# A hybrid decoder layer on one core: plain blocks by thirds of the tokens, and four PSUM banks for small results

## The chip, the cores and the metric

The kernel runs on one core of a Trainium2 chip. A core has five engines that run side by side: TensorE (PE in the profile; its weight loads are listed apart as PEld), VectorE (DVE), ScalarE (ACT), GpSimd (POOL) and SyncE (SP), which here only issues transfers. Matmul results go to PSUM, which has eight banks of 512 fp32 values for each of 128 partitions; DVE or ACT read them from there into SBUF. The metric is the device time of one execution in microseconds, as the median of repeated runs. Before the change it is 2419.35 us (three runs, 2418.73 to 2423.1).

## The reference

One layer of a decoder for 1024 prompt tokens and 8 sample tokens, 1032 columns in all, with a model width of 1024. Three mixers read one normalized input through one combined projection; their gated sum is merged, and a SwiGLU block follows.

```
sc_b, sc_c, sc_x, z, xbc, dt_raw, q, gates = jnp.split(xn @ w_in, splits, axis=-1)
...
y_a = (sc_b * conv_u) @ w_sc_out
...
y_ssd, ssm_new = ssd_fn(xs, dt, a, bm, cm, ssm_s0)
...
y_b = group_rmsnorm(y_ssd, ssm_norm_w, SSM_GROUPS) @ w_ssm_out
qh = q.reshape(bsz, seq, ATTN_HEADS, ATTN_HEAD_DIM)
scores = jnp.einsum('blhd,bmhd->bhlm', qh, mem_k).astype(jnp.float32) * (ATTN_HEAD_DIM ** -0.5)
probs = jax.nn.softmax(scores, axis=-1).astype(mem_v.dtype)
y_c = jnp.einsum('bhlm,bmhd->blhd', probs, mem_v).reshape(bsz, seq, ATTN_DIM) @ w_attn_o
g_a, g_b, g_c = jnp.split(jax.nn.sigmoid(gates), N_BRANCHES, axis=-1)
merged = g_a * y_a + g_b * y_b + g_c * y_c
return merged @ w_merge_o, (sc_new, ssm_conv_new, ssm_new)
```

`ssd_fn` is a chunked scan over eight chunks of 128 tokens for the prompt and one recurrent step for the sample. The memory attention has 4 heads of width 256 over 256 memory tokens.

## The kernel before

**Blocks.** A block is one group of 128 output features for all 1032 columns, over eight groups of 128 inputs. Operands are split into a high part in the fast format fp32r and the rest (`hi`, `lo`), so a block takes three products for each of the eight inputs: hi x hi, hi x lo, lo x hi. Most large products use a Strassen scheme on halves of the tokens. The *plain* blocks use `gemm` (L199): for each input k and each of the three products, three matmuls go to three PSUM banks, with 260, 512 and 260 columns (`thirds`, L80). One block is thus 72 matmuls into one tile of three banks. The tile comes from `mm_ps` (L63), a pool of two such tiles: six banks. When all inputs are through, one instruction reads all 1032 columns.

**Small results.** The other two banks belong to the pool `psm`, from which `sm_ps` (L66) hands out one bank at a time in turn. All small matmuls and transposes of the scan, of the attention and of the norms use it.

**The stage around the change.** After the projections (span position 979 us) come 40 plain blocks in this order: eight for q (`q_step`, L868; weights named wq0 to wq7), eight each for the outputs 0, 1 and 2 (`out_part`, L1501; wo00 to wo07, wo10 to wo17, wo20 to wo27: w_sc_out and the two halves of w_ssm_out), and eight for w_attn_o (loop from L1854; wo30 to wo37). The scan of four groups runs beside q and the first outputs, the attention and the state outputs beside the rest. They are cut into pieces that stand in a queue, and `tick` (L183) inside `gemm` takes the next piece at marks spread over the eight inputs. So PE gets small work between the matmuls of a block.

In the scan, a piece of `first` (L1046) fills the tiles bp and xp, `second` (L1072) po and py, `third` (L1099) pss. (The blocks of the outputs are also called po in the profile, at L218.) In the attention, `kv_keys` fills pskT, `a_scores` psa, `a_probs` psp, `a_out` psv, `s_out` pso, and `conv_state` pcs. All of them are tiles of `sm_ps`.

**What reads a block.** For q, ACT scales the result into an SBUF tile (L872). For output 0, DVE multiplies it by a gate (L1517); for output 1, ACT copies it (L1521) and issues its store; for output 2, DVE adds what output 1 left (L1524) and multiplies by the gate (L1525). For w_attn_o, DVE multiplies by the gate (L1872) and adds to `merged` (L1873).

**Seams.** Outputs 0, 1, 2 and w_attn_o read different inputs. In the last block before each such change a callback, `between` (L1494), loads the next inputs and splits them (L177 on ACT, L178 on DVE; tiles b00h, b00l to b07h, b07l) as the old ones come free; `out_in` (L1480) does the rest in front of the first block. The tiles are shared with the inputs in use and with those of the scan: twelve for the high parts and twelve for the low ones.

**What sets the order.** Within each engine instructions run in one fixed order. It is laid out when the program is built: a scheduler takes, of those instructions that it estimates to be ready, the first in program order, and it hands out the tiles of a pool as they come free in its estimate. On the chip, an engine waits at an instruction whose input or tile is not ready, and all that follows on that engine waits with it.

**After the blocks.** The merge products begin (loop L1967, matmuls at L1949). For the pair m = 0 the tiles pa and pb are three-bank tiles of `mm_ps` and pc is made of two small banks (`pieces`, L1939, against `whole`, L1935); `onto` (L1954) adds a product to x2, with one DVE instruction for `whole` and two for `pieces`.

Of the kernel before, what the change touches and what calls it, by code (L numbers as in the profile page):

```python
# [9 lines left out]
F32 = mybir.dt.float32  # L10
# [7 lines left out]
P = 128  # L18
# [25 lines left out]
def tile_kernel(ctx: ExitStack, tc, a, o):  # L44
# [18 lines left out]
    def mm_ps(name):  # L63
        return pmm[0].tile([P, NCH, 512], F32, tag="mm", name=name)

    def sm_ps(name):  # L66
        return psm.tile([P, 512], F32, tag="sm", name=name)

    def dram(name, shape):
        return dp.tile(shape, F32, tag=name, name=name)  # L70
# [6 lines left out]
    def flat(ps):  # L77
        return ps.rearrange("p n c -> p (n c)")[:, 252 : 252 + TT]
# [120 lines left out]
    def gemm(w, acts, name, width=P, off=0):  # L199

        hi, lo = w
        ps = mm_ps(name)
        nk = len(acts)
        n = int(pace[0] + pace[1])
        pace[1] += pace[0] - n
        marks = [nk * i // n for i in range(n)]
        between = seam.pop() if seam else None
        for k, (ah, al) in enumerate(acts):
            if between is not None:
                between(k)  # L210
            if k == 1 and owed:
                owed.pop()()
            for _ in range(marks.count(k)):
                tick()
            ks = slice(k * width + off, k * width + off + P)
            for i, (wt, x) in enumerate(((hi, ah), (hi, al), (lo, ah))):
                for po, xc in thirds(ps, x):
                    PE.matmul(po, wt[:, ks], xc, start=(k == 0 and i == 0), stop=(k == nk - 1 and i == 2))  # L218
        return ps

    def wblock(w, col):
        return w[:, col : col + P].rearrange("(k p) c -> p k c", p=P)
# [585 lines left out]
    def proj(col, name):  # L808
        return gemm(weights(wblock(w_in, col), "w" + name), xn, "ps_" + name)
# [57 lines left out]

    def q_step(i):  # L868
        def s():
            ps = proj(C_Q + i * P, f"q{i}")  # L870
            t = ev_tile(f"q{i}")
            S.activation(t[:, :TT], flat(ps), AF.Copy, scale=QS)  # L872
            G.tensor_copy(qs[:, i, :], t[:, T:TT])
            S.dma_start(q_d[i], t[:, :TT])

        return [Step(wblock(w_in, C_Q + i * P), f"wq{i}", s)]
# [581 lines left out]
    st_stack.close()  # L1458
    pa_stack.close()
    ch_stack.close()  # L1460
    pmm[0] = mm_stack.enter_context(tc.tile_pool(name="pmm1", bufs=2, space=PSUM))

# [38 lines left out]
    def out_part(i, m, w, src, nxt):  # L1501


        nm = f"{i}{m}"
        if m == 0:
            out_in(src)
        if i != 1:
            gt = ev_tile(f"gt{nm}")
            SY.dma_start(gt[:, :TT], gt_d[(0, 8, 8)[i] + m])
        if i == 2:  # L1510
            t = ev_tile(f"yr{nm}")
            SY.dma_start(t[:, :TT], yr_d[m])
        if m == KD - 1:
            out_ahead(nxt)
        ps = gemm(weights(wblock(w, m * P), f"wo{nm}"), acts, f"po{nm}")
        if i == 0:
            V.tensor_mul(gt[:, :TT], flat(ps), gt[:, :TT])  # L1517
            owed.append(lambda: SY.dma_start(mg_d[m], gt[:, :TT]))
        elif i == 1:
            t = ev_tile(f"yr{nm}")  # L1520
            S.copy(t[:, :TT], flat(ps))  # L1521
            S.dma_start(yr_d[m], t[:, :TT])
        else:
            V.tensor_tensor(t[:, :TT], flat(ps), t[:, :TT], op=ALU.add)  # L1524
# [313 lines left out]
    def form_t2(kt):  # L1838
        t1, b12, b21, b22 = quarters(kt)
        V.tensor_sub(t1, t1, b22)  # L1840
        mform("nT2", kt, t1)
# [9 lines left out]
        mform("T4", kt, t2)  # L1851

    wm = [wblock(a["w_merge_o"][0], m * P) for m in range(KD)]
    for m in range(KD):  # L1854
# [17 lines left out]
        V.tensor_mul(gt[:, :TT], flat(ps), gt[:, :TT])  # L1872
        V.tensor_add(merged[m], merged[m], gt[:, :TT])  # L1873
        if m < 4:
            form_t1(m)
# [90 lines left out]
    S.activation(ln1, ones[:, 0:1], AF.Ln)  # L1966
    for m in (0, 2):  # L1967
        nm = f"wm{m}"
        raw1, raw2, sa, wA, wS = begun if m == 0 else st_begin(wm[m], wm[m + 1], nm, ev_sums)
# [456 lines left out]
```

## Time and profile before

| What | Value |
|---|---|
| Median of three runs | 2419.35 us (2418.73 to 2423.1) |
| The profiled execution | 2420.07 us |
| Its span, first to last instruction | 2418.3 us |
| Mean granted clock of PE | 0.998 |
| Scan beside plain blocks | 979 to about 1335 us |
| Attention beside plain blocks | about 1335 to 1560 us |
| Rest of w_attn_o alone | to 1643 us |

A row of the waits names an engine, what it was about to run, what it waited for, and then the total in us, the number of times and the longest wait. A row of the chain of waits is a start, a length and the work that set the end at that time. A row of a tile lists an engine's instruction on that tile with its count, its shortest, median and longest duration in ns, and the starts of the first and the last. A row of the timeline is a start, a duration, an instruction, and in brackets the idle time before it with what ended it. In names, buffer numbers are left out, and the part behind the arrow is what is read.

### The profile page before, as it was taken

The page shows a single profiled execution, that of the slowest core. Times are in us where ns is not written, and L with a number is a line of the kernel's source. Part 1 is how long each engine was busy: PE and PEld are TensorE (multiplying, and loading weights), DVE is VectorE, ACT ScalarE, POOL GpSimd, SP SyncE. Part 2 cuts the span into 40 slices and gives each one's busy share as a digit, 9 for nine tenths or more (in the row PEclk, how much of TensorE's full clock was granted, in tenths as well). Part 3 has the DMA queues.
Part 4 walks back from the last instruction along what each step waited for, and adds up shares of the span by engine and source line. Part 5 has one row for each costly group of instructions (what it writes and reads, how often), then busy time and mean ns, then how long its engine had stood idle before and what let it go on. Part 6 is the DMA issues. An engine that isn't in the chain of part 4 may idle for free.

```text
span 2418.3 us, 45032 instructions
## 1 busy us (share of the span) xinstructions
PE 2386.4 (99%) x18620; PEld 2268.5 (94%) x18620; DVE 1644.9 (68%) x2666; ACT 1098.9 (45%) x1762; POOL 106.0 (4%) x163
## 2 busy tenths in 40 slices
PE   8999999999999999999999999999999999999998
PEld 6999999999999999888888887899999999999998
DVE  6744677777777676568688773469687655567965
ACT  6633555455453543656555542214553333343423
POOL 0000000000000000212112000000000000000000
PEclk9999999999999999999999999999999999999999
DMA  6444423444354345768886796764345333355622
GB/s 210 132 154 161 136 83 115 141 141 132 108 160 118 106 132 171 231 214 271 261 283 216 255 338 222 269 231 145 117 160 174 98 102 105 93 179 154 194 90 78
DMA packets 348244, 403.74 MB, mean 167 GB/s; under 512 B 16014, under 2 KB 269054, under 8 KB 348031
## 3 DMA queue, kind: packets, MB, share of 16 engines
q1 hardware_dynamic: 324902, 337.60, 45.0%
q10 hardware_dynamic: 23137, 63.26, 6.9%
q8 instruction: 146, 2.39, 0.4%
q14 instruction: 59, 0.48, 0.1%
HBM read 284.65 MB, written 116.38 MB: 166 GB/s over the span
## 4 chain that ended last, share of the span: by engine, by line
PE 91%; DVE 3%; DMA 3%; ACT 1%; issue 1%; SPq 0%; DVEq 0%; ACTq 0%
PE po L218 12%; PE ps_q L218 3%; PE pd L2237 1%; PE pss L1103 1%; PE py L1090 1%; PE ps_z L218 1%; DMA in<-yb_d 1%; PE po L1082 1%; PE G16m L269 1%; PE d00m L269 1%; PE Z2m L269 1%; PE Z14m L269 1%; PE G22m L269 1%; PE X18m L269 1%; PE Z8m L269 1%; PE Z10m L269 1%
## 5 line engine op out<-in xcount | busy, mean ns | idle before, releaser
L1034 ACT ACTIVATE r<-r,acum 128x128 f32<-128x128 f32 x256 | 79.3, 391 | 3.3 <-DMA r<-ac_d 2.4
L823 DVE SCALAR_TENSOR_TENSOR ax<-u,prm,ax 128x1024 f32<-128x1024 f32 x44 | 56.3, 1280 | 0.0
L975 ACT ACTIVATE st<-st,es 128x128 f32<-128x128 f32 x128 | 41.4, 392 | 21.1 <-DMA st<-in_state_ssm_dram 16.6
L1067 POOL TENSOR_TENSOR xdd<-xdt,decst 128x512 f32<-128x512 f32 x32 | 34.4, 1074 | 284.1 <-DVE xdt L1063 278.3
L1061 DVE TENSOR_TENSOR r<-r,cbm 128x1024 f32<-128x1024 f32 x32 | 39.1, 1223 | 4.3 <-ACT r L1036 2.4
L1086 DVE TENSOR_TENSOR y<-po,ea 128x512 f32<-128x512 f32 x28 | 19.3, 690 | 31.6 <-PE po L1082 31.6
L977 DVE SCALAR_TENSOR_TENSOR st<-sr,dts,st 128x128 f32<-128x128 f32 x128 | 40.4, 347 | 0.4
L1524 DVE TENSOR_TENSOR yr<-po,yr 128x1032 f32<-128x1032 f32 x8 | 9.9, 1232 | 40.6 <-PE po L218 40.6
L1103 PE MATMUL pss<-xdd,bT 128*128 128x512 f32 x64 | 34.4, 619 | 2.3 <-ACT bT L1060 1.8
L981 DVE SCALAR_TENSOR_TENSOR sr<-st,sr 128x128 f32<-128x128 f32 x128 | 35.4, 286 | 1.1
L1090 PE MATMUL py<-r,xdt 128*64 128x128 f32 x512 | 35.0, 279 | 0.0
L1036 ACT ACTIVATE r<-r 128x1024 f32<-128x1024 f32 x32 | 33.8, 1057 | 0.7
L1116 POOL TENSOR_TENSOR s<-s,cdec 128x512 f32<-128x512 f32 x28 | 33.2, 1186 | 0.6 <-DVE s L1109 0.4
L1090 PEld LDWEIGHTS py<-r,xdt 128*64 128x64 f32 x512 | 27.3, 136 | 4.4 <-issue 1.0
L1082 PE MATMUL po<-bc,s 128*128 128x128 f32 x224 | 29.6, 275 | 0.0
L1082 PEld LDWEIGHTS po<-bc,s 128*128 128x128 f32 x224 | 28.0, 191 | 1.0
L1639 ACT ACTIVATE pr<-psa,mx 128x256 f32<-128x256 f32 x32 | 14.9, 471 | 30.4 <-DVE mx L1637 30.4
L826 DVE SCALAR_TENSOR_TENSOR ax<-u,prm,ax 128x1032 f32<-128x1032 f32 x22 | 28.3, 1287 | 0.0
L820 ACT ACTIVATE ax<-u,prm 128x1024 f32<-128x1024 f32 x22 | 27.4, 1246 | 1.2 <-ACT u L902 0.4
L1063 DVE TENSOR_TENSOR xdt<-xp,dtT 128x512 f32<-128x512 f32 x32 | 21.9, 684 | 8.8 <-PE xp L1056 8.8
L1627 DVE SCALAR_TENSOR_TENSOR kc<-kc,qb 128x256 f32<-128x256 f32 x64 | 23.7, 418 | 4.7 <-DMA qb<-qs_d 4.7
L1060 ACT COPY bT<-bp 128x128 f32<-128x128 f32 x32 | 8.4, 261 | 38.8 <-DVE cbm L1058 38.7
(8855 smaller groups left out, 8937.9 us busy)
## 6 DMA issues: line engine op xcount, KB each, us to landing
r<-ac_d SPq DMA_DIRECT2D x32, 512.0 KB
gt_d<-G ACTq DMA_DIRECT2D x24, 516.0 KB
gt<-gt_d SPq DMA_DIRECT2D x24, 516.0 KB
xs_d<-ax ACTq DMA_DIRECT2D x22, 516.0 KB
zs<-zs_d SPq DMA_DIRECT2D x16, 516.0 KB
yb_d<-x SPq DMA_DIRECT2D x16, 516.0 KB
in<-yb_d SPq DMA_DIRECT2D x16, 516.0 KB
st<-in_state_ssm_dram SPq DMA_DIRECT2D x32, 256.0 KB
```

The source lines that it names most:

```text
L218: PE.matmul(po, wt[:, ks], xc, start=(k == 0 and i == 0), stop=(k == nk - 1 and i == 2))
L269: last_mm[0] = PE.matmul(po, wt[:, ks], xc, start=(start and kt == 0 and i == 0), stop=(kt == 3 and i == 2), skip_group_check=True,).ins
L823: V.scalar_tensor_tensor(acc[:, :T], u[:, j : j + T], w[j], acc[:, :T], op0=ALU.mult, op1=ALU.add)
L975: S.activation(st[:, i], st[:, i], AF.Copy, scale=es[:, g * 4 + i, b : b + 1])
L977: V.scalar_tensor_tensor(st[:, i], rb, dts[:, g * 4 + i, b : b + 1], st[:, i], op0=ALU.mult, op1=ALU.add)
L981: V.scalar_tensor_tensor(rb, st[:, i], 1.0, rc, op0=ALU.mult, op1=ALU.mult, accum_out=ys[:, g * 4 + i, b : b + 1],)
L1034: S.activation(r[:, j, :], r[:, j, :], AF.Relu, scale=-1.0, bias=acum[:, c, h : h + 1])
L1061: V.tensor_tensor(r, r, bc(cbm.unsqueeze(1), [P, HPG, P]), op=ALU.mult)
L1067: G.tensor_tensor(b3(xdd, HPG), b3(xdt, HPG), bc(decst[:, c, hs].unsqueeze(2), [P, HPG, 64]), op=ALU.mult)
L1082: PE.matmul(po[:, t * P : (t + 1) * P], state["s"][:, t * P : (t + 1) * P], bcg[1][:, cs], start=True, stop=True,)
L1090: PE.matmul(py[hp : hp + 64, (h // 2) * P : (h // 2 + 1) * P], xdt[:, h * 64 : (h + 1) * 64], r[:, (h % 2) * 4 + h // 2, :], start=True, s ...
L1103: PE.matmul(pss, bT, xdd, start=True, stop=True)
```

## The change

The plain blocks of q, of the three outputs and of w_attn_o go through a new function, `gemm3`. It takes one tile of one bank for each third of 344 columns, from a pool of four banks, and calls `out` for a third as soon as all its inputs are through. With `lag` at its default of 8 the thirds run one after the other; with a lag of 1 they run side by side, each one input behind the one before. The lag is 1 in the first and last block of each output and in the first of w_attn_o. Ticks are spread over 24 steps in place of eight, and `between` is called in front of the steps of the last third. The two banks that are left go to a second small pool, and `sm_ps` alternates between both.

What reads a block now does so by thirds. In the last block of w_attn_o, the addition of yg, the first weights of the merge and six of its forms are issued from the callback of the first third. For the pair m = 0 of the merge, pa is made of the two old small banks; then the plain pools are closed, and a pool of two three-bank tiles gives pc and pb. For m = 2, pa is a three-bank tile and pc is made of small banks, as before, with pc now taken together with pa.

```diff
+    ring = {"main": None, "small": None, "n": 0}
+
     def sm_ps(name):
-        return psm.tile([P, 512], F32, tag="sm", name=name)
+        ring["n"] += 1
+        pool_ = ring["small"] if ring["small"] is not None and ring["n"] % 2 else psm
+        return pool_.tile([P, 512], F32, tag="sm", name=name)
+
+    def plain_pools(n):
+        for key, bufs in (("main", 4), ("small", 2)):
+            ring[key] = mm_stack.enter_context(tc.tile_pool(name=f"p{key}{n}", bufs=bufs, space=PSUM))
...
+    def gemm3(w, acts, name, out, lag=KD):
+
+        hi, lo = w
+        nk = len(acts)
+        pss = [ring["main"].tile([P, 512], F32, tag="mm", name=f"{name}_{t}")[:, :CW] for t in range(NCH)]
+        n = int(pace[0] + pace[1])
+        pace[1] += pace[0] - n
+        marks = [NCH * nk * i // n for i in range(n)]
+        between = seam.pop() if seam else None
+        order = [(t, m - t * lag) for m in range(nk + (NCH - 1) * lag) for t in range(NCH) if 0 <= m - t * lag < nk]
+        for step, (t, k) in enumerate(order):
+            if between is not None and t == NCH - 1:
+                between(k)
+            if step == 3 and owed:
+                owed.pop()()
+            for _ in range(marks.count(step)):
+                tick()
+            ks = slice(k * P, (k + 1) * P)
+            c = slice(t * CW, (t + 1) * CW)
+            ah, al = acts[k]
+            for i, (wt, x) in enumerate(((hi, ah), (hi, al), (lo, ah))):
+                PE.matmul(pss[t], wt[:, ks], x[:, c], start=(k == 0 and i == 0), stop=(k == nk - 1 and i == 2))
+            if k == nk - 1:
+                out(t, c, pss[t])
...
-            ps = proj(C_Q + i * P, f"q{i}")
             t = ev_tile(f"q{i}")
-            S.activation(t[:, :TT], flat(ps), AF.Copy, scale=QS)
+            gemm3(
+                weights(wblock(w_in, C_Q + i * P), f"wq{i}"), xn, f"ps_q{i}",
+                lambda n, c, ps: S.activation(t[:, c], ps, AF.Copy, scale=QS),
+            )
...
-    pmm[0] = mm_stack.enter_context(tc.tile_pool(name="pmm1", bufs=2, space=PSUM))
+    plain_pools(1)
...
-        ps = gemm(weights(wblock(w, m * P), f"wo{nm}"), acts, f"po{nm}")
+        if i == 1:
+            t = ev_tile(f"yr{nm}")
+
+        def part(n, c, ps):
+            if i == 0:
+                V.tensor_mul(gt[:, c], ps, gt[:, c])
+            elif i == 1:
+                S.copy(t[:, c], ps)
+            else:
+                V.tensor_tensor(t[:, c], ps, t[:, c], op=ALU.add)
+
+        gemm3(weights(wblock(w, m * P), f"wo{nm}"), acts, f"po{nm}", part, 1 if m in (0, KD - 1) else KD)
...
-        ps = gemm(w, acts, f"po3{m}")
-        V.tensor_add(merged[m], merged[m], yg[:, :TT])
-        if m == KD - 1:
-            begun = st_begin(wm[0], wm[1], "wm0", ev_sums)
-            for kt in range(3):
-                form_t2(kt)
-            for kt in range(3):
-                mform("B21", kt, merged[kt + 4][:, HS[0]])
-        V.tensor_mul(gt[:, :TT], flat(ps), gt[:, :TT])
+
+        def part(n, c, ps):
+            if n == 0:
+                V.tensor_add(merged[m], merged[m], yg[:, :TT])
+                if m == KD - 1:
+                    begun.append(st_begin(wm[0], wm[1], "wm0", ev_sums))
+                    for kt in range(3):
+                        form_t2(kt)
+                    for kt in range(3):
+                        mform("B21", kt, merged[kt + 4][:, HS[0]])
+            V.tensor_mul(gt[:, c], ps, gt[:, c])
+
+        gemm3(w, acts, f"po3{m}", part, KD if m else 1)
...
-        pa, pb = (whole(mm_ps(nm + n)) for n in "ab")
-        pc = pieces(nm + "c")
+        if m == 0:
+            ring["small"] = None
+            pa = pieces(nm + "a")
+        else:
+            pa, pc = whole(mm_ps(nm + "a")), pieces(nm + "c")
         m_prod(pa, wA, 0, "B11", True)
         onto(m, 0, pa)
+        if m == 0:
+            mm_stack.close()
+            pmm[0] = mm_stack.enter_context(tc.tile_pool(name="pmm2", bufs=2, space=PSUM))
+            pc = whole(mm_ps(nm + "c"))
+        pb = whole(mm_ps(nm + "b"))
```

More of the change, by code (lines that the diff above doesn't have):

```diff
@@ L1514, in out_part @@
             out_ahead(nxt)
-        ps = gemm(weights(wblock(w, m * P), f"wo{nm}"), acts, f"po{nm}")
+        if i == 1:
[8 more added lines that the diff above has]
+        gemm3(weights(wblock(w, m * P), f"wo{nm}"), acts, f"po{nm}", part, 1 if m in (0, KD - 1) else KD)
         if i == 0:
-            V.tensor_mul(gt[:, :TT], flat(ps), gt[:, :TT])
             owed.append(lambda: SY.dma_start(mg_d[m], gt[:, :TT]))
         elif i == 1:
-            t = ev_tile(f"yr{nm}")
-            S.copy(t[:, :TT], flat(ps))
             S.dma_start(yr_d[m], t[:, :TT])
         else:
-            V.tensor_tensor(t[:, :TT], flat(ps), t[:, :TT], op=ALU.add)
             V.tensor_mul(t[:, :TT], t[:, :TT], gt[:, :TT])
@@ L1853, in tile_kernel @@
     wm = [wblock(a["w_merge_o"][0], m * P) for m in range(KD)]
+    begun = []
     for m in range(KD):
@@ L1863, in tile_kernel @@
         SY.dma_start(gt[:, :TT], gt_d[16 + m])
-        ps = gemm(w, acts, f"po3{m}")
-        V.tensor_add(merged[m], merged[m], yg[:, :TT])
-        if m == KD - 1:
-            begun = st_begin(wm[0], wm[1], "wm0", ev_sums)
-            for kt in range(3):
-                form_t2(kt)
-            for kt in range(3):
-                mform("B21", kt, merged[kt + 4][:, HS[0]])
-        V.tensor_mul(gt[:, :TT], flat(ps), gt[:, :TT])
+        def part(n, c, ps):
[9 more added lines that the diff above has]
+        gemm3(w, acts, f"po3{m}", part, KD if m else 1)
         V.tensor_add(merged[m], merged[m], gt[:, :TT])
@@ L1968, in tile_kernel @@
         nm = f"wm{m}"
-        raw1, raw2, sa, wA, wS = begun if m == 0 else st_begin(wm[m], wm[m + 1], nm, ev_sums)
+        raw1, raw2, sa, wA, wS = begun[0] if m == 0 else st_begin(wm[m], wm[m + 1], nm, ev_sums)
         residuals(m)
-        pa, pb = (whole(mm_ps(nm + n)) for n in "ab")
-        pc = pieces(nm + "c")
+        if m == 0:
[3 more added lines that the diff above has]
+            pa, pc = whole(mm_ps(nm + "a")), pieces(nm + "c")
         m_prod(pa, wA, 0, "B11", True)
         onto(m, 0, pa)
+        if m == 0:
[3 more added lines that the diff above has]
+        pb = whole(mm_ps(nm + "b"))
         wT = st_split(st_adds2(raw1, raw2, sa, nm, ev_sums), nm + "T")
```

## The prediction

> **What bounds the kernel now.** I read the page first, then the busy time by stage, then the waits of TensorE in the stage that the change touches.
>
> ```profile
> span 2418.3 us, 45032 instructions
> PE 2386.4 (99%) x18620; PEld 2268.5 (94%) x18620; DVE 1644.9 (68%) x2666; ACT 1098.9 (45%) x1762; POOL 106.0 (4%) x163
> ...
> PE 91%; DVE 3%; DMA 3%; ACT 1%; issue 1%; SPq 0%; DVEq 0%; ACTq 0%
> ```
>
> TensorE carries the chain for 91% of the span. A change can only win where TensorE waits, or by making its work shorter. By stage (columns: stretch, length, then busy time of PE, PEld, DVE, ACT, POOL, granted clock, DMA):
>
> ```profile
> 979.00:1335.00 356.00, 350.75 (x2475) 297.04 (x2475) 257.96 (x309) 205.75 (x408) 71.20 (x68) 1.00 0.76 244
> 1335.00:1560.00 225.00, 217.60 (x1461) 189.21 (x1460) 124.83 (x289) 85.12 (x173) 0.00 (x0) 1.00 0.78 269
> 1560.00:1643.00 83.00, 83.00 (x531) 75.34 (x530) 58.54 (x65) 20.42 (x27) 0.00 (x0) 1.00 0.66 221
> 1643.00:1686.00 43.00, 43.00 (x361) 42.90 (x360) 38.87 (x59) 19.70 (x29) 0.00 (x0) 1.00 0.51 167
> ```
>
> These are the scan, the attention, the eight blocks of w_attn_o, and the first merge products. Only in the first two is TensorE idle, for 356.00 - 350.75 + 225.00 - 217.60 = 12.7 us. The waits there, by what ended them, first of the matmuls and then of the weight loads (total, times, longest):
>
> ```profile
> PE pcs L1575 <- ACT ot L1756: 1.9, 1, 1.9
> PE psa L1721 <- ACT pr L1639: 1.8, 1, 1.8
> PE pss L1103 <- ACT bT L1060: 1.8, 2, 1.1
> PE xp L1056 <- DMA x<-xs_d: 1.6, 3, 0.8
> PE pskT L1606 <- ACT qrows L1240: 1.2, 1, 1.2
> PE psp L1735 <- DVE pr L1645: 1.2, 1, 1.2
> PE pso L1677 <- DMA vc<-in_cache_mem_v_dram: 0.9, 1, 0.9
> PE pskT L1606 <- DVE kTl L1609: 0.9, 2, 0.5
> PE psp L1735 <- DVE pTl L1743: 0.7, 1, 0.7
> PE pss L1103 <- DVE y L1086: 0.5, 1, 0.5
> ```
> ```profile
> PEld pcs L1575 <- ACT ot L1756: 2.4, 1, 2.4
> PEld psa L1721 <- ACT pr L1639: 2.2, 2, 2.1
> PEld pskT L1606 <- ACT qrows L1240: 1.6, 2, 1.5
> PEld pskT L1606 <- DVE kTl L1609: 1.5, 2, 0.8
> ```
>
> The reader is to sort the ten rows by what the waiting matmul needed. Six were waiting for an engine that reads an older small result, so for one of the two small banks: pcs behind the copy of psv into ot, psa behind the exponential that reads an older psa, pskT twice, psp behind pTl, pss behind y. Four were waiting for data: bT, x, pr and vc.
>
> **The change, part by part.** *Small results through four banks.* It takes away the bank waits. Bounds: 1.9 + 1.8 + 1.2 + 0.9 + 0.7 + 0.5 = 7.0 us by the matmul rows; with the weight-load rows for the first four, which begin earlier because the load waits too, 2.4 + 2.2 + 1.6 + 1.5 + 0.7 + 0.5 = 8.9 us. The load has to be done before its matmul, so I take 8.9. Not all of it stays: behind the psa wait the same attention head next needs pr, a data row above, so of its 2.2 us I count half. That leaves 7.8 us. From the other side nothing may stay (0, each wait turned into one for data), and if the shorter reads of the large banks also relieve the data rows (1.8 + 1.6 + 1.2 + 0.9 = 5.5 us), 14.4 us go.
>
> *Matmuls of 344 columns in place of 260, 512 and 260.* The count stays at 72 a block, 40 blocks (8 q, 24 of the outputs, 8 of w_attn_o). No 344-column matmul of this type runs before; its neighbours do:
>
> ```profile
> 397.67 20.02 PE X2m L269 x168
> ...
> 1541.38 101.40 PE po L218 x643
> ```
> ```profile
> 1399.94 0.23 PE psv L1753
> ...
> 1402.47 0.24 PE psv L1755
> ```
> ```profile
> 2390.82 0.18 PE pl L2385
> ...
> 2396.62 0.17 PE pl L2385
> ```
>
> One matmul costs 101.40 / 643 = 157.7 ns now (mean width 344), 20.02 / 168 = 119.2 ns at 258 columns, (2396.62 - 2390.82) / 33 = 175.8 ns at 384 (34 in a row), and (1402.47 + 0.24 - 1399.94) / 12 = 230.8 ns at 512. Between 258 and 384, 344 columns come to 157.8 ns; between 258 and 512, to 157.0. Over 2880 matmuls that is +0.3 or -2.0 us; I take 0. The twelve psv matmuls write one bank six times in a row without paying for it, so 24 in a row should not either.
>
> *Three reads of a block's result in place of one.*
>
> ```profile
> L1086 DVE TENSOR_TENSOR y<-po,ea x28: 677/692/693, 997.7 to 1307.0; 128x512 f32<-128x512 f32 x28
> L1521 ACT COPY yr<-po x8: 1011/1016/1038, 1288.1 to 1423.1; 128x1032 f32<-128x1032 f32 x8
> L1524 DVE TENSOR_TENSOR yr<-po,yr x8: 1226/1232/1234, 1435.5 to 1552.1; 128x1032 f32<-128x1032 f32 x8
> ```
>
> On DVE 1232 - 692 = 540 ns for 520 columns leaves 160 ns fixed, so 344 columns take 517 ns and three of them 319 ns more than one of 1032. Over 24 blocks (outputs 0 and 2, w_attn_o) DVE works 7.7 us longer; ACT, with at most the same fixed part, 16 x 0.32 = 5.1 us (outputs 1 and q). Both engines have room in these stages, so on the path: 0. Without that room, up to 12.8 us. The last third is read in 0.52 us instead of 1.23 us.
>
> *The merge.* Its first product goes to the two small banks, and six new banks are opened behind the last block. The first T1 product must wait until the last third is read, 0.52 us after the block, while the B11 product covers about 24 x 119.2 ns = 2.9 us. Four additions onto x2 become two halves and one becomes whole: three more fixed parts, 0.5 us of DVE, in a stage where DVE is busy 38.87 of 43.00 us. I take 0; bounds -0.3 and +0.5 us. Moving st_begin and the forms into the first third's callback leaves their order on DVE, ACT and SP as it was; the first two multiplications only join that queue early.
>
> *The seams.* Plain blocks now own four banks instead of six. In the blocks where the inputs change (m = 7 and 0) all three thirds are open at once, so only one bank is left for the next block. And q7 goes third by third, so xn is released only from its last third on.
>
> ```profile
> L218 PE MATMUL po<-b07h,wo17l x3: 280/287/400, 1416.2 to 1416.5; 128*128 128x260 f32 x2, 128*128 128x512 f32 x1
> ```
> ```profile
> 1418.46 1.05 ACT L177 CAST b03h<-in 128x1032 fp32r<-128x1032 f32 x1 [3.29 <-DMA in<-yb_d]
> ...
> 1423.06 1.01 ACT L1521 COPY yr<-po 128x1032 f32<-128x1032 f32 x1
> ```
> ```profile
> L218 PE MATMUL po<-b02l,wo31h x3: 283/283/396, 1561.5 to 1563.2; 128*128 128x260 f32 x2, 128*128 128x512 f32 x1
> ```
> ```profile
> L218 PE MATMUL po<-b07h,wo30l x3: 277/284/393, 1567.2 to 1567.5; 128*128 128x260 f32 x2, 128*128 128x512 f32 x1
> ```
> ```profile
> L218 PE MATMUL ps_q<-xnh,wq7h x24: 280/364/796, 1106.2 to 1127.9; 128*128 128x260 f32 x16, 128*128 128x512 f32 x8
> ```
> ```profile
> L178 DVE TENSOR_TENSOR b00l<-in,b00h x4: 1221/1234/1234, 1114.5 to 1550.8; 128x1032 fp32r<-128x1032 f32 x4
> ...
> L218 PE MATMUL po<-b00h,wo00h x3: 281/285/401, 1131.1 to 1131.4; 128*128 128x260 f32 x2, 128*128 128x512 f32 x1
> ```
> ```profile
> 1120.00:1130.00 10.00, 10.00 (x82) 8.49 (x83) 10.00 (x12) 5.75 (x8) 5.16 (x4) 1.00 1.01 385
> ```
>
> From outputs 1 to 2: block wo17 ends at 1416.5, and its copy starts only at 1423.06, behind casts that wait for DMA. Today a third block would need that bank. Now the second third of wo20 needs a bank that this queue frees. Bounds: 0, if the thirds' copies are queued ahead of the casts, and 1423.06 + 1.01 - 1416.5 - 0.95 (the six matmuls of its first third that go before) = 6.6 us. The copies of the first two thirds come due before the block ends, ahead of most casts, so I take 1.0. To w_attn_o: while its inputs arrive, TensorE fills with wo31, three inputs deep (27 matmuls) before wo30 ends at 1567.5. With one spare bank only 9 of the 27 can run; the other 18 x 157.7 ns = 2.8 us would be idle. No wait of po for an input stands in today's rows, so I take a value nearer to the other end, 0.5. From q to outputs 0: the split of the first input moves from 1114.5 to about 1106.2 + 2/3 x (1131.1 - 1106.2) = 1122.8, into a DVE that is busy 10.00 of 10.00 us. Four splits of 1.22 us pushed behind make at most 4.9 us; scan pieces can run instead, so 0.5. Together 2.0 us, bounds 0 and 14.3.
>
> Sum: -7.8 + 0 + 0 + 0 + 2.0 = -5.8 us. The profiled execution took 2420.07 us, 1.8 us around its span; that is 2414.3 us. It lies 0.7 us above the median of 2419.35 us, so on the scale of the runs 2413.6 us.
>
> **The rivals.** *No change.* The bank waits turn into waits for data, since the order was laid out for an earlier end of each reader. For it: four of the ten rows are such waits already. Against it: the longest row, pcs, needs nothing but its bank. If its 2.4 us alone are gained and the 2.0 us of the seams lost, the time is 2419 us.
>
> *Slower.* TensorE stands at the wo20 seam because ACT reads wo17's thirds behind casts that wait for DMA. With the 2.8 us at w_attn_o, half of the q seam (2.4 us) and only pcs and pskT gained, which need nothing but a bank (2.4 + 1.6 + 1.5 = 5.5 us): 2419.35 + 6.6 + 2.8 + 2.4 - 5.5 = 2425.7 us. Beside those two seams it decides as soon as it lasts over 0.3 us; alone, from 5.5 us on. For it: the copy at 1423.06 is that late today. Against it: two of the three reads are due earlier than the one read now.
>
> *A slow clock behind that stall.* The Trainium skill, TensorE: Matmul & The Clock Gate (HAM oscillation — how this bites in real kernels), warns against gaps over about 3.4 us because the clock then falls to half. Here waits of up to 2.4 us left the granted clock at 1.00, so no run shown goes that far.
>
> ```profile
> 0.00:20.00 20.00, 12.91 (x61) 11.20 (x61) 11.58 (x39) 11.55 (x23) 1.05 (x8) 0.83 0.95 318
> ```
>
> The only low clock is at the start: 0.83 over 20 us, a loss of 3.4 us. Once more behind the stall of 6.6 us, it gives 2425.7 + 3.4 = 2429.1 us.
>
> **How the numbers follow.** Forecast 0.44 (of it 0.08 for a gain beyond the sum, when data waits shrink as well: down to 2419.35 - 14.4 = 2405 us); no change 0.26; slower 0.27; slower with the low clock 0.03. The forecast's own range is 2405 to 2416. The range for 8 in 10 starts at 2404 and reaches over both slower cases to 2429. A difference of 0.2%, 4.8 us, is about what a measurement here tells from none: below 2414.5 faster, above 2424.2 slower. Faster 0.44, same 0.26, slower 0.30.
>
> **What would show it.** Right: the six bank rows are gone from the waits of TensorE and the four data rows are about as large; idle time of TensorE in the two stages near 5 us; 40 blocks of 72 matmuls still at 157 to 158 ns. The chain at wo20, w_attn_o and wo00 shows gaps below 1 us each. Wrong: a wait of po for ACT yr or a cast at wo20, a wait of po for b0xl at wo30 or wo00, or a longer product time in the merge. A matmul of 344 columns at 160 ns would by itself cost 2880 x 2.3 ns = 6.6 us and undo the gain.

## The result, and the profile after

| | Median | Range |
|---|---|---|
| Before | 2419.78 us (6 runs) | 2417.84 to 2423.1 |
| After | 2429.99 us (6 runs) | 2426.74 to 2432.16 |

The ratio is 1.0038, with a 95% interval of 1.0025 to 1.0051: the change makes the kernel 9 us slower by the ratio, 10 us by the medians. The profiled execution took 2426.74 us, the fastest of the six, so the traces show 6.7 us of it (a span of 2425.0 against 2418.3 us).

The page of the changed kernel, first two lines:

```profile
span 2425.0 us, 45119 instructions
PE 2395.5 (99%) x18620; PEld 2314.7 (95%) x18620; DVE 1648.8 (68%) x2717; ACT 1102.1 (45%) x1794; POOL 115.6 (5%) x163
```

TensorE has as many instructions as before, but it is busy 9.1 us longer. The next view (stretch, length, then busy time of PE, PEld, DVE, ACT, POOL, granted clock, DMA) takes two stretches of each kernel: from the first q matmul to the last of w_attn_o, and from there to the first product of the second half of the merge (wm4). Before:

```profile
979.06:1642.50 663.44, 650.86 (x4459) 561.10 (x4459) 440.80 (x660) 310.75 (x606) 71.20 (x68) 1.00 0.76 250
1642.50:1682.91 40.41, 40.41 (x338) 40.30 (x337) 36.74 (x56) 18.56 (x28) 0.00 (x0) 1.00 0.51 166
```

After:

```profile
980.46:1644.47 664.01, 657.99 (x4461) 606.01 (x4461) 442.19 (x703) 312.42 (x635) 80.97 (x68) 1.00 0.75 249
1644.47:1688.78 44.31, 41.15 (x339) 40.56 (x338) 39.56 (x64) 19.80 (x31) 0.00 (x0) 1.00 0.50 162
```

In the first stretch TensorE's idle time falls from 12.6 to 6.0 us: the gain is there. But its busy time grows by 7.1 us, and the stretch ends up 0.6 us longer. The second stretch grows by 3.9 us. The rest of the 6.7 us is 1.4 us ahead of the change, in code that is the same (an experiment that is also unchanged there, x2, is 1.7 us late at that point), and 0.8 us behind wm4.

The waits of TensorE's matmuls after the change (what it was about to run, what it waited for, total, times, longest):

```profile
PE po L250 <- DVE gt L1555: 2.0, 1, 2.0
PE wm2a L1996 <- DVE x L2004: 1.6, 1, 1.6
PE po L250 <- ACT yr L1557: 0.8, 1, 0.8
PE wm2a L1996 <- ACT mT42h L453: 0.8, 1, 0.8
PE wm0a L1996 <- issue: 0.8, 1, 0.8
PE xp L1091 <- DMA x<-xs_d: 0.7, 3, 0.4
PE po L250 <- DVE b00l L186: 0.7, 1, 0.7
PE po L250 <- ACT b06h L185: 0.6, 1, 0.6
PE pskT L1648 <- DMA kk<-k_d: 0.5, 1, 0.5
...
PE po L250 <- ACT b04h L185: 0.2, 1, 0.2
```

All six bank waits are gone, and three of the four data waits with them; the fourth, xp for x, falls from 1.6 to 0.7 us. New are waits of the plain blocks (po at L250) for the readers of older thirds and for inputs, and waits in the merge.

Where the busy time grew, the groups of TensorE's instructions say (instructions, then busy us and mean ns). Before, in the first stretch:

```profile
L1090 PE MATMUL py<-r,xdt 128*64 128x128 f32 x512 | 35.0, 279 | 0.0
L1082 PE MATMUL po<-bc,s 128*128 128x128 f32 x224 | 29.6, 275 | 0.0
```

After:

```profile
L1125 PE MATMUL py<-r,xdt 128*64 128x128 f32 x512 | 43.1, 282 | 0.0
L1117 PE MATMUL po<-bc,s 128*128 128x128 f32 x224 | 31.5, 283 | 0.0
```

By their rows the same matmuls take 8.1 + 1.9 = 10.0 us more. Neighbouring groups overlap at their ends, so this overstates it somewhat: the stretch as a whole is 7.1 us busier. One piece of each on the timeline (start, duration) shows why. Before:

```profile
1011.14 1.06 PE L1082 MATMUL po<-bc,s 128*128 128x128 f32 x8
1012.12 1.09 PE L1090 MATMUL py<-r,xdt 128*64 128x128 f32 x16
1013.15 0.63 PE L218 MATMUL ps_q<-xnh,wq1h 128*128 128x260 f32 x2
```

After:

```profile
1095.01 0.87 PE L1125 MATMUL py<-r,xdt 128*64 128x128 f32 x10
1095.80 1.16 PE L1117 MATMUL po<-bc,s 128*128 128x128 f32 x8
1096.89 0.65 PE L1125 MATMUL py<-r,xdt 128*64 128x128 f32 x6
1097.47 0.33 PE L1087 MATMUL bp<-ident,bc 128*128 128x128 f32 x1
```

A py matmul has weights of 64 columns (128*64 in its form), and the trace starts such matmuls in pairs, 6 to 7 ns apart, with 103 ns to the next pair. Unbroken, po and py take 1013.15 - 1011.14 = 2.01 us; with po in the middle of py, 1097.47 - 1095.01 = 2.46 us, so 0.45 us more. From the last po matmul to the first of py the starts are 205 ns apart, and about as much at the other two switches; inside po they are 112 ns apart. In the rows of py this happens in 19 of 32 pieces after the change (19 x 0.45 = 8.6 us) and in none before. The Trainium skill, TensorEngine Tiling (Array Packing), Key Properties, states that a change of tiling mode drains TensorE. The longer steps agree with that and give its price here; the drain itself no row shows.

### The profile page after: what moved, and what is told of

The parts are those of the page before. It is cut to its first block, busy times and chain, and to the rows that moved or that the text cites. A ratio compares the mean times of both kernels' runs of the same rounds, so it can differ in the third digit from the quotient of the medians.

```text
span 2425.0 us, 45119 instructions
## 1 busy us (share of the span) xinstructions
PE 2395.5 (99%) x18620; PEld 2314.7 (95%) x18620; DVE 1648.8 (68%) x2717; ACT 1102.1 (45%) x1794; POOL 115.6 (5%) x163
## 4 chain that ended last, share of the span: by engine, by line
PE 89%; DVE 5%; DMA 4%; ACT 1%; issue 1%; SPq 0%; DVEq 0%; ACTq 0%
PE po L250 11%; PE ps_q L250 3%; PE py L1125 2%; PE pd L2292 1%; PE po L1117 1%; PE pss L1138 1%; PE ps_z L226 1%; PE G16m L302 1%; PE d00m L302 1%; PE d10m L302 1%; PE Z2m L302 1%; PE Z14m L302 1%; PE X4m L302 1%; PE d06m L302 1%; PE d04m L302 1%; PE d02m L302 1%
## 5 line engine op out<-in xcount | busy, mean ns | idle before, releaser
L1102 POOL TENSOR_TENSOR xdd<-xdt,decst 128x512 f32<-128x512 f32 x32 | 39.8, 1242 | 270.9 <-DVE xdt L1098 268.7
L1559 DVE TENSOR_TENSOR yr<-po,yr 128x344 f32<-128x344 f32 x24 | 12.2, 514 | 51.2 <-PE po L250 45.2
L1125 PE MATMUL py<-r,xdt 128*64 128x128 f32 x512 | 43.1, 282 | 0.0
L1095 ACT COPY bT<-bp 128x128 f32<-128x128 f32 x32 | 8.4, 263 | 46.9 <-DVE cbm L1093 46.9
L1917 DVE TENSOR_TENSOR gt<-po,gt 128x344 f32<-128x344 f32 x24 | 12.0, 512 | 22.7 <-PE po L250 21.5
```

The source lines that it names most:

```text
L1102: G.tensor_tensor(b3(xdd, HPG), b3(xdt, HPG), bc(decst[:, c, hs].unsqueeze(2), [P, HPG, 64]), op=ALU.mult)
L1125: PE.matmul(py[hp : hp + 64, (h // 2) * P : (h // 2 + 1) * P], xdt[:, h * 64 : (h + 1) * 64], r[:, (h % 2) * 4 + h // 2, :], start=True, s ...
```

## The experiments

Fifteen kernels ran, each timed in five rounds against the kernel before on the same chip. The ratio is to that kernel; 0.001 is 2.42 us. By the intervals, a difference between two runs is known to within 0.0012 to 0.0018, some 3 to 4 us; smaller differences between single runs are not told apart.

| Run | Median, us | Ratio, 95% interval |
|---|---|---|
| the change | 2429.99 | 1.0038, 1.0025 to 1.0051 |
| x1 merge as before | 2427.26 | 1.0033, 1.0020 to 1.0045 |
| x2 before, banks of the new merge | 2420.8 | 1.0000, 0.9991 to 1.0009 |
| x3 six main, two small banks | 2433.71 | 1.0057, 1.0044 to 1.0069 |
| x4 four main, two small | 2432.89 | 1.0059, 1.0046 to 1.0073 |
| x5 lag 1 in wo37 | 2425.86 | 1.0021, 1.0011 to 1.0031 |
| x6 six main, two small, lag 0 | 2421.9 | 1.0009, 1.0000 to 1.0017 |
| x7 five main, three small | 2424.46 | 1.0015, 1.0006 to 1.0024 |
| x8 lag 1 everywhere | 2436.22 | 1.0065, 1.0052 to 1.0078 |
| x9 py unbroken | 2424.95 | 1.0018, 1.0009 to 1.0026 |
| x10 x9 and lag 1 in wo37 | 2423.66 | 1.0010, 1.0001 to 1.0019 |
| x11 x7, py unbroken | 2417.39 | 0.9988, 0.9979 to 0.9997 |
| x12 before, py broken by hand | 2436.3 | 1.0060, 1.0048 to 1.0073 |
| x13 x10 and lag 1 in q7 | 2421.29 | 1.0001, 0.9992 to 1.0010 |
| x14 x3 with lag 1 in q7, wo37 | 2424.86 | 1.0018, 1.0009 to 1.0027 |
| x15 x11 with lag 0 everywhere | 2422.98 | 1.0007, 0.9998 to 1.0016 |

The expectations place a wait of po for gt at wo10. That place is wrong: the timeline has it in front of the second third of wo01.

**x1 and x2: is it the merge's layout?** x1 goes back to the old order of the program there (for wo37 the addition of yg, the forms and then the three multiplications, all from the last third's callback) and to the old bank shapes; x2 is the kernel before with the new shapes alone.

```diff
 x1
+            hold.append((c, ps))
+            if n < (NCH - 1 if m == KD - 1 else 0):
+                return
...
+            while hold:
+                c, ps = hold.pop(0)
+                V.tensor_mul(gt[:, c], ps, gt[:, c])
...
         if m == 0:
             ring["small"] = None
-            pa = pieces(nm + "a")
+            mm_stack.close()
+            pmm[0] = mm_stack.enter_context(tc.tile_pool(name="pmm2", bufs=2, space=PSUM))
+        pa, pb = (whole(mm_ps(nm + n)) for n in "ab")
+        pc = pieces(nm + "c")
 x2
-        pa, pb = (whole(mm_ps(nm + n)) for n in "ab")
-        pc = pieces(nm + "c")
+        if m == 0:
+            pa = pieces(nm + "a")
...
+            mm_stack.close()
+            pmm[0] = mm_stack.enter_context(tc.tile_pool(name="pmm2", bufs=2, space=PSUM))
+            pc = whole(mm_ps(nm + "c"))
+        pb = whole(mm_ps(nm + "b"))
```

> The changed kernel, with the end of w_attn_o and the start of the merge as before: the three multiplications of wo37 stand behind its forms again, and for m = 0 pa and pb are three-bank tiles and pc two small banks. Theory 'merge' (the stretch from the first merge product to wm4 lost 3.9 us because DVE is held by wo37's early multiplications and pa shares two small banks with its readers): some 3.5 us come back, 2426.5 us; the stretch from wm0's first product to wm4's first is within 0.5 us of the kernel before (40.3 us). Rival 'seams' (the loss is in waits of po for readers and inputs, the merge only shows a delay inherited from before it): within 1 us of 2430, and the stretch stays near 44 us.

> The kernel before, with the merge's banks alone as in the change: for m = 0 pa in two small banks, then the pool of three-bank tiles closed and opened again for pc and pb. Theory 'merge, by its banks': 2 to 4 us slower than before, 2422 to 2424 us, with new waits of the merge's products. Rival 'merge, by DVE's queue' (the early multiplications of wo37 are what costs, and they are not in this kernel): within 0.7 us of the kernel before, 2419 to 2420.5 us.

x2 is the kernel before to within 0.0009 either way, and its stretch is 40.85 us (40.41 before): the bank shapes cost nothing that the times show. x1 did not bring the stretch back (44.13 us, at a mean granted clock of 0.96), so its first theory is not the cause. Its rival has the stretch right, but not the cause, as x5 shows below. Three ACT rows show what it left in place: the first cast of the form nT2, with the idle time ahead of it, before the change, after it, and in x1.

```profile
1632.90 1.15 ACT L420 CAST mnT20h<-mg 128x516 fp32r<-128x516 f32 x2 [0.78 <-PE po L218]
```
```profile
1641.51 1.15 ACT L453 CAST mnT20h<-mg 128x516 fp32r<-128x516 f32 x2 [7.09 <-PE po L250]
```
```profile
1644.60 1.15 ACT L453 CAST mnT20h<-mg 128x516 fp32r<-128x516 f32 x2 [7.09 <-PE po L250]
```

In the last two, ACT stands 7.09 us until matmuls of wo37 let go of the tile that the cast writes. Before the change the casts began 1642.50 - 1632.90 = 9.6 us ahead of wo37's last matmul; after it, 1644.47 - 1641.51 = 3.0 us. With the thirds one after the other, every input of wo37 is still needed in its last third.

**x3 and x4: what do the banks do?** Each changes one line.

```diff
-        for key, bufs in (("main", 4), ("small", 2)):
+        for key, bufs in (("main", 6),):      x3
+        for key, bufs in (("main", 4),):      x4
```

> The changed kernel with six single banks for the thirds of the plain blocks and the two old small banks alone. Theory 'seams, by four main banks' (waits of po for the readers of earlier thirds come from the pool being one bank from empty): the rows of po waiting for gt, yr of the older block go (about 4 us), the bank waits of the small results (pcs, psa, pskT, psp: 7 to 9 us) come back, and the time is 2431 to 2436 us. Rival 'small banks give nothing' (what they free comes back as waits for data): the bank waits come back but the data waits shrink as much, and the time is 2424 to 2428 us.

> The changed kernel without the two additional small banks (two banks stay unused): four main banks, two small ones. Theory 'small banks gain': against the changed kernel it loses what they gave, 6 to 9 us, so 2436 to 2439 us, and pcs, psa, pskT and psp wait for their banks again. Rival 'small banks give nothing': within 2 us of 2430, and the data waits of the scan (py for xdt, bT, x) are smaller by what the bank waits are larger.

x3 falls into the range of its first theory, x4 between both. But x3 tells against the theory's reason: six main banks are no faster than four (x4), and both are some 14 us slower by the ratio than the kernel before with the same two small banks. Something else in the thirds costs more than the banks.

**x5, x6, x8: the order of the thirds.** x6 has six main and two small banks, x8 four and four.

```diff
 x5
-        gemm3(w, acts, f"po3{m}", part, KD if m else 1)
+        gemm3(w, acts, f"po3{m}", part, 1 if m in (0, KD - 1) else KD)
 x6, in gemm3
+        lag = 0
 x8, in gemm3
+        lag = 1
```

> The changed kernel with a lag of 1 in the last block of w_attn_o (wo37) too; nothing else. Theory 'late release' (with the thirds one after the other every input tile of wo37 is held until the last third; ACT stood 7.1 us idle in front of the cast mnT20h, so all forms of the merge begin 6.6 us later than before): the idle time before that cast falls below 1 us, mnT20h starts again more than 6 us before wo37's last matmul, the stretch from wo37's last matmul to wm4's first one falls from 44.3 to 40.4 to 41 us, and the time is 2426 to 2427 us. Rival 'DVE has too much to do' (three multiplications of wo37 and the halves of x2 in place of whole ones fill DVE): the stretch stays at 43.5 to 44.5 us and the time at 2429 to 2431 us.

> The changed kernel with six single banks for the plain blocks, the two old small banks alone and a lag of 0: for each input all three thirds, as before, and three reads at the end of each block. Against the run with six banks and a lag of 8 (2433.7 us) only the order of the matmuls differs, against the kernel before (2420 us) only columns, reads and marks. Theory 'the order costs' (thirds one after the other release the inputs late, and the inputs of the last block of each kind most of all): 2419 to 2423 us, with the merge's stretch at 40.4 to 41 us and q's eight blocks at 152 to 153 us. Rival 'the thirds cost' (more reads, other places of the small work, whatever the order): 2429 us or more, q's blocks at 155 us or more.

> The changed kernel with a lag of 1 in every plain block: inputs are released as the block goes, but a block opens its second and third third 0.95 and 2.4 us after its start and needs banks whose last matmul is only 3.3 us old (21 matmuls of 158 ns). Theory 'late release': as with wo37 alone, and q's eight blocks back at 152 to 153 us: 2423 to 2426 us, if DVE and ACT read a third within 3.3 us. Rival 'the bank of an older third decides': new waits of po for gt, yr and ps_q's readers in many blocks, each 0.3 to 1.5 us, 5 to 15 us in all: 2431 to 2440 us.

x5 confirms the late release, with one part of it missed: ACT waits 1.89 us in place of 7.09 (below 1 was expected), the cast leads wo37's last matmul by 8.1 us, and the stretch is 41.07 us again.

```profile
1636.78 1.15 ACT L453 CAST mnT20h<-mg 128x516 fp32r<-128x516 f32 x2 [1.89 <-PE po L250]
```
```profile
1644.91:1685.98 41.07, 40.41 (x339) 40.20 (x339) 36.21 (x60) 17.57 (x26) 0.00 (x0) 1.00 0.54 174
```

x6 against x3 is the order of the thirds alone: 1.0057 to 1.0009, or 11.6 us. It is the largest single cost in the change. In the profiled executions, 8.1 us of it lie in the two stretches: 669.69 and 43.70 us in x3, 664.39 and 40.93 us in x6. Against the kernel before, x6 has all that the thirds bring but the order, at a ratio of 1.0009: the reads, the columns and the marks cost some 2 us (0 to 4 by the interval). q's eight blocks took 154.7 us there and not the 152 to 153 expected. x8 went to its rival. Its longest wait, and the granted clock behind it:

```profile
1432.81 0.66 PE L251 MATMUL po<-b00h,wo20h 128*128 128x344 f32 x1 [5.03 <-ACT yr L1558]
```
```profile
1427.00:1433.00 6.00, 0.97 (x6) 0.68 (x6) 3.00 (x3) 3.74 (x6) 0.00 (x0) 0.92 0.82 274
1433.00:1438.00 5.00, 5.00 (x20) 5.00 (x21) 4.02 (x4) 3.54 (x6) 0.00 (x0) 0.50 0.91 267
```

This is the stall at wo20 that the prediction named, with the clock at half for 5 us behind it: by 5.00 x (1 - 0.50), another 2.5 us.

**x7: five and three banks,** with a lag of 1 in q7 and wo37.

```diff
-        for key, bufs in (("main", 4), ("small", 2)):
+        for key, bufs in (("main", 5), ("small", 1)):
-        pool_ = ring["small"] if ring["small"] is not None and ring["n"] % 2 else psm
+        pool_ = ring["small"] if ring["small"] is not None and ring["n"] % 3 == 0 else psm
```

> The changed kernel with five single banks for the plain blocks and three small ones (one added to the two old ones), and a lag of 1 in q7 and wo37 too. Theory 'late release' with 'four main banks': the merge's 3.5 us come back, the waits of po for gt at wo10 and for yr at wo20 (2.0 and 0.8 us) fall below 0.5 us, the small results lose no more than 1.5 us to the third bank, q7's release is early again: 2422 to 2425 us. Rival 'the seams cost nothing beyond noise': only the merge's 3.5 us, less what the missing bank costs (1 to 3 us): 2427 to 2429 us.

2424.46 us is inside the first range, and the waits for gt and yr are gone. But the first stretch is still as long as before the change, though TensorE is idle for 7.0 us in it against 12.6:

```profile
979.43:1643.02 663.59, 656.62 (x4460) 604.90 (x4461) 446.28 (x707) 314.81 (x640) 90.54 (x68) 1.00 0.76 250
```

So the loss is in the busy time, and in py: 41.0 us, with 14 of 32 pieces broken.

**x9 to x12: the broken heads.** x9 to x11 put py behind po; x12 is the kernel before with three heads of py, po, then five heads; py takes its bank ahead of po there.

```diff
-                    PE.matmul(
+                    last_po = PE.matmul(
...
+            with tc.issue_after(last_po.ins) if c > 0 else nullcontext():
                 for h in range(HPG):
                     hp = (h % 2) * 64
                     PE.matmul(
```

> The changed kernel with the matmuls of py ordered behind the last one of po in each piece of the scan, so that the 16 of a py run unbroken; nothing else. Theory 'broken heads' (with four small banks the order laid out breaks the 16 py matmuls into 6 and 10 around po in 19 of 32 pieces; TensorE is busy 10.0 us longer with py and po, 0.53 us for each break): py and po are busy 35 and 29.6 us again, and the time is 2420 to 2423 us. Rival 'the order only shows waits' (TensorE begins py early because it would wait for po's bank or state anyway): the busy time falls but idle time for po and the state takes its place, and the time is 2427 to 2431 us.

> As the run with unbroken heads, with a lag of 1 in wo37 too. Theories 'broken heads' and 'late release' together: 4 us below the run with unbroken heads and 7 to 10 us below the one with the lag alone (2425.9 us), so 2416 to 2419 us, faster than the kernel before. Rival 'they overlap' (what one gives back the other would have hidden): 2420 us or more.

> As the run with five and three banks (lag of 1 in q7 and wo37, 2424.5 us), with the heads unbroken; there 14 of 32 pieces were broken. Theory 'broken heads': 14 x 0.53 = 7 us less, 2417 to 2418.5 us. Theory 'four main banks' says in addition that the waits of po for gt at wo10 and for yr at wo20 stay away, so it should be 1 to 2 us below the run with four and four banks. Rival: the three small banks cost as much as the seams gain, within 1 us of that run.

> The kernel before, with the heads broken by hand in all 28 pieces that have a po: three heads of py, then po's four matmuls, then five heads. All banks, blocks and reads as before. Theory 'broken heads': 28 x 0.53 = 15 us slower if each break costs what it did in the changed kernel, 2430 to 2436 us, with py busy 46 to 48 us in place of 35. Rival 'the order only shows waits': within 3 us of 2420 us, since TensorE then starts py earlier.

x12 decides it: it is 16.5 us slower by the order of py and po alone. TensorE's idle time in the stretch is no longer for it, 10.1 against 12.6 us. Its groups:

```profile
L1084 PE MATMUL py<-r,xdt 128*64 128x128 f32 x512 | 46.9, 284 | 0.0
L1095 PE MATMUL po<-bc,s 128*128 128x128 f32 x224 | 30.0, 277 | 0.0
```

(46.9 - 35.0 + 30.0 - 29.6) / 28 = 0.44 us busy for each break, and 16.5 / 28 = 0.59 us of time. Not all of the 16.5 us need be breaks: behind a wait of 2.29 us for pcs the clock stood at 0.66 for 5 us, some 1.7 us. In x9 the busy time is back:

```profile
L1126 PE MATMUL py<-r,xdt 128*64 128x128 f32 x512 | 35.0, 279 | 0.5 <-DVE xdt L1098 0.5
L1117 PE MATMUL po<-bc,s 128*128 128x128 f32 x224 | 30.1, 277 | 0.5 <-DVE s L1145 0.5
```

But x9 gains 5 us, not 7 to 10, and x10 stays 5 us above its range. Waits took a part, as the rivals had it: in the first stretch TensorE is busy for 651.64 in place of 657.99 us, but idle for 11.4 in place of 6.0. From x9's waits, and its clock behind the second one, which ends at 1336.6:

```profile
PE po L250 <- DVE gt L1556: 3.2, 1, 3.2
PE psa L1764 <- ACT q00h L185: 2.9, 1, 2.9
```
```profile
1337.00:1342.00 5.00, 5.00 (x25) 5.00 (x24) 5.00 (x5) 1.82 (x2) 0.00 (x0) 0.66 0.99 397
```

The attention reached its first scores before ACT had cast q: 2.9 us, and 5.00 x (1 - 0.66) = 1.7 us of clock. x11 keeps 0.3 us of the second and nothing of the first. From x7 it differs by the order of py behind po alone and is 1.0015 to 0.9988, or 6.5 us, faster: 0.47 us for each of the 14. Its 2417.39 us are in the range of its first theory, and it is faster than the kernel before:

```profile
982.37:1639.06 656.69, 649.58 (x4461) 602.96 (x4462) 448.41 (x707) 313.40 (x640) 94.70 (x68) 1.00 0.76 252
1639.06:1680.27 41.21, 40.37 (x339) 40.16 (x339) 36.53 (x60) 17.56 (x26) 0.00 (x0) 1.00 0.54 174
```

**x13 to x15: what is left.** x13 is x10 with q7's lag, so x11 with four and four banks; x14 is x3 with both lags; x15 is x11 with a lag of 0.

```diff
 x13, x14
                 lambda n, c, ps: S.activation(t[:, c], ps, AF.Copy, scale=QS),
+                1 if i == KD - 1 else KD,
 x15, in gemm3
+        lag = 0
```

> As the run with five and three banks and unbroken heads (2417.4 us), but with four and four banks; q7 and wo37 have a lag of 1 here too. It differs from the run of 2423.7 us (unbroken heads, lag in wo37 alone) by q7's lag alone, and from the one of 2417.4 us by the banks alone. Theory 'four main banks': within 1.5 us of 2423.7 us, with the waits of po for gt at wo10 (2.8 us) and yr at wo20 (1.6 us) still there. Rival 'q7's late release': within 1.5 us of 2417.4 us.

> As the run with six main and two small banks (2433.7 us), with a lag of 1 in q7 and wo37 too. The same banks with a lag of 0 everywhere took 2421.9 us. Theory 'late release in the last blocks': those two blocks make up the difference but for the merge's share, 2422 to 2426 us. Rival 'the order costs in all blocks' (also the blocks between hold their inputs, and the reads of three thirds come at other times): only the merge's 3 us, 2429 to 2432 us, with the waits of xp for x still near 5.9 us.

> As the run with five and three banks and unbroken heads (2417.4 us), with a lag of 0 in all blocks. A block's third third then needs, 0.95 us after its start, the bank of the older block's first third, whose last matmul ended 0.95 us before the block did: 1.9 us for its read. Theory 'the order costs in all blocks': 2413 to 2416 us, as the inputs are released early everywhere. Rival 'the bank of an older third decides': new waits of po for gt, yr and q's reads in many of the 40 blocks, 0.2 us and more each, 2424 us and more.

x13 lies between its two theories: q7's lag is worth 2.2 us (1.0010 to 1.0001), five and three banks 3.1 us (1.0001 to 0.9988). The intervals do not tell the first from nothing, and the second only just. The wait for gt that was to stay went with q7's lag alone: in the changed kernel it stood in front of wo01, and DVE's timeline shows the splits of the new inputs, released late by q7, from 1129 to 1143 us, and then work of the scan and its norm up to that multiplication.

```profile
1152.57 0.51 DVE L1555 TENSOR_TENSOR gt<-po,gt 128x344 f32<-128x344 f32 x1
```
```profile
1153.13 0.42 PE L250 MATMUL po<-b00h,wo01h 128*128 128x344 f32 x1 [1.96 <-DVE gt L1555]
```

What x13 keeps and x11 lacks is the wait for q00h:

```profile
1335.40 0.58 PE L1765 MATMUL psa<-kTh,q00h 128*128 128x256 f32 x1 [2.92 <-ACT q00h L185]
```

So the 3.1 us may be the other order that the attention got as much as a spare main bank; no run parts the two. x14 is right by its first theory: the lags of two blocks give 9.4 us (1.0057 to 1.0018), most of the 11.6 us of the order, though xp waits 5.8 us for x as before. x15 came out below its rival's 2424 us but nearer to it, 4.6 us slower than x11; two waits stand out, not many: po waited 2.8 us for yr and 1.5 us for gt.

## Why the prediction was wrong

It forecast 2413.6 us, with a range to 2429; 2429.99 us came out, on the other side of no change. By the ratios, these runs lead from the kernel before to the changed one, each step known to some 2 to 4 us:

| Step | From, to | us |
|---|---|---|
| Thirds, input by input | before, x6 | +2.2 |
| Order of the thirds | x6, x3 | +11.6 |
| Two main banks fewer | x3, x4 | +0.5 |
| Two small banks more, heads unbroken | x4, x9 | -9.9 |
| Heads broken | x9, the change | +4.8 |

The gain from the banks came, at about the size forecast (7.8 us). Two steps of the prediction failed: it put the order of the thirds at 0 in the merge and 0.5 us behind q, and it had no term for another order of the small matmuls. By its own steps:

- **Bank waits, -7.8 us: right as a wait, incomplete as a term of the sum.** The rows went as listed, and idle time in the two stages fell to 5.4 us, where "near 5" was named. That the four data rows would stay about as large was wrong: three of them went too. The step that failed is the bound "from the other side nothing may stay (0)": it let waits turn only into waits, and held that the small matmuls themselves stay as they are. With banks free earlier, the order laid out at build time put po into the middle of py, some 9 to 10 us of busy time, of which 4.8 us of time come back when the order is pinned (x9). That the banks are the reason is shown by x3 and x4 (two small banks, no break) and x7 (three, 14 breaks); that the scheduler took po because it stands earlier in the program is argued, not shown. With the heads unbroken the term has about its size: the 9.9 us from x4 to x9.
- **Matmuls of 344 columns, 0: right.** A row of the chain has 76 of them in 11.95 us, 157.2 ns each.

```profile
1162.17 11.95 PE po L250 x76
```

- **Three reads, 0 on the path, 517 ns each: right in size.** The path is not shown apart: with the rest of the thirds they cost the 2.2 us of x6.

```profile
L1559 DVE TENSOR_TENSOR yr<-po,yr 128x344 f32<-128x344 f32 x24 | 12.2, 514 | 51.2 <-PE po L250 45.2 <-DMA yr<-yr_d 5.7
```

- **The merge, 0 (bounds -0.3 and +0.5): failed, +3.9 us.** It weighed bank shapes and the queue order, and by x2 the shapes rightly at nothing. It missed that wo37 with a lag of 8 keeps its inputs, whose tiles the forms take over; a lag of 1 there gives 4.1 us back (x5). For q7 the prediction had the same release in its sum; for wo37, the block with the same default, it did not ask.
- **Seams, +2.0 us: too small.** The rows of po add up to 2.0 + 0.8 + 0.7 + 0.6 + 0.2 = 4.3 us. wo20 was near (0.8 for 1.0), w_attn_o higher (1.5 for 0.5), q to outputs 2.0 us for 0.5, and one block later than expected, at a bank and not at an input. With six main and two small banks, q7's and wo37's lags together are worth 9.4 us (x14); with four and four banks and heads unbroken, q7's alone is worth 2.2 us (x13), which the intervals do not tell from nothing.
- **The slower rival** named 2425.7 us with the stall at wo20. In the changed kernel that stall is 0.8 us, and the clock behind it stays at 1.00. So the sign came from other causes, and it is chance that the case with the low clock, 2429.1 us, lies within 1 us of the result. The stall itself is real, as x8 shows.

From the change to x11 the ratios form a chain: -4.8 us for unbroken heads (x9), -1.9 for wo37's lag (x10; 4.1 in x5, from the change itself), -2.2 for q7's lag (x13), -3.1 for five and three banks (x11). That leaves the kernel 0.12% below the one before (0.03 to 0.21%).

## What to carry to other kernels

Where a scheduler orders the instructions, a freed buffer changes the order as well as the waits: compare busy time by group, not idle time alone, and pin with an explicit dependency those runs that are dear to interrupt. Before a loop is turned so that parts run one after the other, ask for the last block before each change of inputs when its inputs are let go of, and what takes their tiles. Undo a change by its parts: here one part was worth some 10 us, and the other parts hid it.

## What the hardware showed

A switch between matmuls with weights of 128 columns and of 64 costs: 0.44 us of TensorE's busy time where a run of sixteen is broken once (x12).

The clock can fall after a gap of less than 3 us. In x9, 2.92 us without matmuls brought it to 0.66 over the next 5 us, in x10 2.83 us to 0.50:

```profile
1152.05 0.66 PE L250 MATMUL po<-b00h,wo01h 128*128 128x344 f32 x1 [2.83 <-DVE gt L1556]
```
```profile
1152.00:1157.00 5.00, 4.95 (x13) 4.00 (x14) 2.93 (x5) 0.83 (x1) 0.00 (x0) 0.50 1.02 360
```

The Trainium skill, TensorE: Matmul & The Clock Gate (HAM oscillation — how this bites in real kernels), sets the limit at about 3.4 us; by these rows a gap under 3 us is enough. By 5.00 x (1 - clock), such a stall costs 1.6 (x9) to 1.9 times (x10) what its row says. The length alone does not decide: the clock stayed at 1.00 behind 1.96 us in the changed kernel and behind 2.47 us in x6 and in x14, and fell to 0.66 behind 2.29 us in x12. What else decides, no run here shows.
